# A decoder trunk on one core: three of eight weight chunks are split by other engines

## The chip, the cores and the metric

The kernel runs on one core of a Trainium2 chip. The metric is the device time of one launch in microseconds (us). A core has a matrix engine (PE, with its weight loads shown apart as PEld), a vector engine (DVE), an activation engine (ACT), a general engine (POOL), and queues that only issue DMAs (SP; ACT and POOL can issue them too). Each engine runs its own list of instructions in order, and waits on semaphores for the others.

## The reference, cut to what matters

Two layers of a decoder for 256 tokens of width 2048, all in float32. One wide projection feeds three token mixers (latent attention, a spatial gating unit, gated linear attention), whose outputs are gated, projected and merged, and projected once more onto the residual:

```
h = rms_norm(x, norm_g);  proj = h @ w_in          # 2048 -> 14416 columns
y_a, y_b, y_c = three mixers, each times silu(z)   # 1024 columns each
merged = sum_b sigmoid(gate_b) * (y_b @ w_branch[b])
x = x + merged @ w_out
```

Nearly all of the work is a product of 256 token rows with a weight matrix that is read from memory once. The precision asked for is float32's.

## The kernel before, in words

Tokens are the rows of every product: 256 tokens are two tiles of 128 (`t` = 0, 1). Weights stream past them. The host lays all weights out as one sequence of **chunks** of 128 partitions x 1024 float32 (512 KB): two contraction tiles of 128 rows by 512 output columns. There are 636 such chunks, 318 in a layer, and four narrow ones of 128 x 768. A block (`block`, L191) is one output stripe of 512 columns, made of 8 chunks (2 or 4 where the contraction is shorter).

PE multiplies in the reduced type float32r. So each chunk is split in two parts whose sum is the float32 value (`Weights.chunk`, L48): SP loads `wraw` (L64); ACT writes `whi`, the rounded value (L65); DVE writes `wlo = wraw - whi` (L66). The tokens are split in the same manner. Each contraction tile and token tile then takes three matmuls, L207 (high x high), L208 (token high x `wlo`) and L209 (token low x `whi`), so a chunk is 12 matmuls of 512 columns. L207 is first, so `whi` is needed first and `wlo` one matmul later.

The buffers rotate: four `wraw`, three `whi`, three `wlo`. `whi` of a chunk can be written when PE has finished the chunk three places before; `wraw` can be loaded when the subtraction of the chunk four places before is done.

A scheduler writes each engine's list in advance. The split is emitted with a high priority (`SPLIT_OFF`), so it stands ahead of other work in the lists of ACT and DVE. The rest (attention, transposes, the scan) is emitted in small steps between the products of a block (`step`), so that its latency is hidden behind them. POOL has little to do: the power that makes a reciprocal square root (`rsqrt`, L126, results `r_x`, `r_c`, `r_q`, `r_k`, `r_v`, `r_o`), and a few DMAs: `wa_raw`, `ba`, `vg`, `wsT`, and `x` in and out (L363, L364, L691, L693, L794, L803).

In the order of chunks a layer has the latents (chunks 1 to 16), two narrow chunks, a gate (17 to 32), the products of the latents (33 to 46, whose left operand is `cT`), then queries and keys of the scan (47 to 62, left operand `xT` again), values (63 to 78, the accumulators that become `vc`), and so on to the output projection (287 to 318). The second layer repeats this from chunk 319 on.

Of the kernel before, what the change touches and what calls it, by code (L numbers as in the profile page):

```python
# [9 lines left out]
F32 = mybir.dt.float32  # L10
# [3 lines left out]
ALU = mybir.AluOpType  # L14
# [15 lines left out]

# The tokens' order on the chip: the second half of the sequence runs backwards, so that the
# keys of the two halves' decay blocks fill the two halves of one stationary operand.
_ROWS = np.concatenate([np.arange(P), np.arange(S - 1, P - 1, -1)])

# Column blocks of the input projection, in the order in which they are computed.
_COL = dict(cq=0, ckv=512, kr=1024, za=1088, u=2112, v=3136, zb=4160, qc=5184, kc=5696,
# [3 lines left out]
class Weights:  # L40
    """Streams weight chunks in the order of the packed DRAM tensor and splits each into two
    float32r parts whose sum is the float32 value."""

    def __init__(self, nc, tc, pools, big, small):
        self.nc, self.tc = nc, tc
        self.raw, self.hi, self.lo = pools
        self.big, self.small = big, small
        self.nb = self.ns = 0  # L48

    def chunk(self, kts, ncols):  # L50
        nc, n = self.nc, kts * ncols
        if ncols == 512:
            src = self.big[self.nb]
            self.nb += 1
        else:
            src = self.small[self.ns]
            self.ns += 1
        step = 512 if ncols == 512 and self.nb <= 2 else n
        with self.tc.high_priority(offset=SPLIT_OFF):
            raw = self.raw.tile([P, 1024], F32, tag="wraw", name="wraw")  # L60
            hi = self.hi.tile([P, 1024], F32R, tag="whi", name="whi")
            lo = self.lo.tile([P, 1024], F32R, tag="wlo", name="wlo")
            for c in (slice(o, o + step) for o in range(0, n, step)):
                nc.sync.dma_start(raw[:, c], src[:, c])  # L64
                nc.scalar.activation(hi[:, c], raw[:, c], AF.Copy)  # L65
                nc.vector.tensor_tensor(lo[:, c], raw[:, c], hi[:, c].bitcast(F32), ALU.subtract)  # L66
        return ([hi[:, k * ncols:(k + 1) * ncols] for k in range(kts)],
                [lo[:, k * ncols:(k + 1) * ncols] for k in range(kts)])
# [3 lines left out]
def trunk(ctx: ExitStack, tc: tile.TileContext, a, out):  # L72
    """The trunk: tokens are the rows of the products, the split weights stream past them."""
    nc = tc.nc
    pool = lambda name, bufs, **k: ctx.enter_context(tc.tile_pool(name=name, bufs=bufs, **k))
    const = pool("const", 1)
    wraw, whi, wlo = pool("wraw", 4), pool("whi", 3), pool("wlo", 3)
    k8, k4, k2 = pool("k8", 12), pool("k4", 8), pool("k2", 5)
# [25 lines left out]

# [1 line left out]
    def load(name, shape, dt=F32):  # L106
# [10 lines left out]
    gains = first_in[:, 0:64].rearrange("p (l i) -> p l i", l=DEPTH)  # L117
    # Per layer: norm_g 0:16, cq_g 16:20, ckv_g 20:24, q_g 24, k_g 25, o_g 26:28.
    def gain(l, i, n=1):
# [11 lines left out]
    def rotary_tables():  # L131
        """cos and sin of positions * inv_freq, times the gains, per layer and for q and k."""
        posf = const.tile([P, NT], F32, name="posf")
# [24 lines left out]
        V.tensor_scalar(cos, cos, -2.0, 1.0, ALU.mult, ALU.add)  # L158
        # tables[l][q or k]: (x1, x2) -> x * TA + swap(x) * TB
        rg = t2("rope_g")[:, 0:256]  # L160
# [12 lines left out]

    # Small work (attention, transposes) is emitted in steps between the products of the blocks,
    # so that its latencies are hidden behind them.
    work, pending = [], set()
# [16 lines left out]

    def block(lhs, kts, before=None):
        """acc[t] = lhs^T @ the next weight block: three products of 12-bit parts."""
        acc = [pA(f"acc{t}") for t in range(NT)]
        for kt in range(0, kts, 2):
# [3 lines left out]
            for k, (wh, wl) in enumerate(zip(hs, ls)):  # L201
# [3 lines left out]
                for t in range(NT):  # L205
                    o, c = acc[t], slice(t * P, (t + 1) * P)
                    nc.tensor.matmul(o, xh[:, c], wh, start=kt + k == 0, stop=False)  # L207
                    nc.tensor.matmul(o, xh[:, c], wl, start=False, stop=False)  # L208
                    nc.tensor.matmul(o, xl[:, c], wh, start=False, stop=kt + k == kts - 1)  # L209
                    step()  # L210
        return acc

    def narrow_block(lhs, kts, ncols):
        """The next narrow weight block, transposed: [ncols, S]."""
        acc = pA("accT")
# [11 lines left out]
    def split(hi, lo, src, scale):  # L227
        """hi + lo = src * scale in float32r parts."""
        act(hi, src, AF.Copy, scale=scale)
        V.scalar_tensor_tensor(lo, src, scale, hi.bitcast(F32), ALU.mult, ALU.subtract)  # L230

    def hl(tiles):
        """Per k-tile (hi, lo, key) of tiles laid out [P, hi/lo, 4, S]."""
        v = [(t.rearrange("p (h k s) -> p h k s", h=2, k=4), id(t)) for t in tiles]
        return [(t[:, 0, k, :], t[:, 1, k, :], of) for t, of in v for k in range(4)]

    def transpose2(src, b):
        """Two transposed 128-column blocks of [P, NT, n]: [128, (block, token)]."""
        p = pB("ptr")
# [6 lines left out]
    def transpose_split(src, scale, name):  # L246
        """[P, NT, 512] token-major -> one k8 tile of 4 k-tiles, split; scale(k) or a number."""
        dst = t8(name, F32R)
# [20 lines left out]

# [1 line left out]
    xT = []  # L271
# [36 lines left out]
    for l in range(DEPTH):  # L308
# [14 lines left out]

# [1 line left out]
        ssr = ts("ssr")  # L325
# [10 lines left out]

# [1 line left out]
        cq8 = t8("cq")  # L338
# [13 lines left out]

# [1 line left out]
        acc = narrow_block(lhs, KT, 96)  # L354
        krT = t2("krT")
        V.tensor_copy(krT[0:64, 0:S], acc[0:64, 0:S])
        # The rank is small: the three products of parts share one contraction.
        arT = sm.tile([96, S], F32R, tag="arT", name="arT", bufs=1)
# [12 lines left out]
        def decay():  # L371
# [9 lines left out]
            for t in range(NT):  # L381
                # log-sigmoid, token-major
                p = pB("pz")
# [11 lines left out]
        def gate_silu(dst):  # L395
            """dst = z (1 + tanh(z rstd / 2)): silu(z rstd) is dst rstd / 2."""
            for j in range(2):
# [9 lines left out]

# [1 line left out]
        lq, lk = hl([cT[0]]), hl([cT[1]])  # L409
# [30 lines left out]

        # rotary: q per head, k once per token
        def rotate(dst, tmp, src, j, shape):
            """dst = src * TA + swap(src) * TB over [P, NT, heads, 64]."""
            TA, TB = tabs[:, l, j, 0], tabs[:, l, j, 1]
# [29 lines left out]
        def attention():  # L474
# [12 lines left out]
            def scores(i, h0):  # L487
                """Exponentials of the masked scores of two heads, whose rotary products fall on the same
                row tile."""
                nk = (i + 1) * P  # L490
# [61 lines left out]

# [1 line left out]
        qk = t8("qk").rearrange("p (j t c) -> p j t c", j=2, t=NT)  # L554
# [5 lines left out]
        for j in range(2):  # L560
            acc = block(lhs, KT)
            for t in range(NT):
# [5 lines left out]

        # diagonal of the attention
        dg = ts("dg", 8)  # L570
# [12 lines left out]
        def gla():  # L583
            yield from pause(4)
            # cumulative decay, feature-major [k, (h, t)]
            for hp in range(2):
# [15 lines left out]
            def factors(lv):  # L602
                """exp(ref - b) k for the keys and exp(b - ref) q for the queries of a level: no
                exponent is positive. Level 0 is the pair of chunks; the others are the pairs of
                halves of blocks within a chunk, the keys of chunk 0 being the first halves and
                those of chunk 1, which runs backwards, the second ones."""
                X = t4("X").rearrange("p (j h s) -> p j h s", j=2, h=4)
# [71 lines left out]

# [1 line left out]
        def gelu(dst, acc, t):  # L681
            """dst = p (1 + tanh(...)): gelu(p rstd) is dst rstd / 2."""
            g2 = t2("g2")
# [63 lines left out]

# [1 line left out]
        gates = {}  # L749
# [34 lines left out]

# [1 line left out]
        lm = hl(mT)  # L786
# [20 lines left out]
def _lay_out(i):  # L807
    """The inputs in the order in which the program reads them; nothing is computed."""
    g = {k: np.asarray(v) for k, v in i.items()}
    big, small = [], []  # L810

    def tiles(w, kts):
        """[K, n] -> chunks [P, kts * n]."""
        k, n = w.shape
# [78 lines left out]
```

## Time and profile before

| what | value |
|---|---|
| median of 2 runs | 1891.13 us (both 1891.13) |
| span of the profiled execution | 1889.1 us |
| PE busy | 1877.6 us, 99% of the span |
| PEld, DVE, ACT, POOL busy | 1547.6, 1097.3, 931.7, 39.6 us |
| memory traffic | 354.19 MB, 187 GB/s over the span |

The page of the profile names no time of its own for the profiled execution but the span from its first to its last instruction, 1889.1 us; the median of the runs lies 2.0 us above it. In the rows below an entry such as "L208 PE MATMUL acc<-wlo,xT" is line, engine, operation, and what it writes from what; buffer numbers are left out of names. A busy time of PE overlaps from one matmul to the next, since they are pipelined, so the pace of matmuls is read from their starts.

### The profile page before, as it was taken

What the parts mean: (1) busy time and instruction counts of PE and PEld (TensorE: products, weight loads), DVE (VectorE), ACT (ScalarE), POOL (GpSimd) and SP (SyncE); (2) the same over time, 40 slices, a digit from 0 to 9 for tenths busy, and PEclk for the clock granted to TensorE, in tenths of its full rate; (3) what the DMA queues carried; (4) which work ended last, traced back from release to release, by engine and by line L of the source; (5) the groups of instructions that cost most, each with busy time, mean ns of one, the idle gap of its engine ahead of it and who ended that gap; (6) DMA issues with size and microseconds to landing.
All of it is one profiled execution on the core that took longest, in us unless ns stands there. A gap on an engine that the chain in (4) does not pass through costs nothing.

```text
span 1889.1 us, 22587 instructions
## 1 busy us (share of the span) xinstructions
PE 1877.6 (99%) x8632; PEld 1547.6 (82%) x8632; DVE 1097.3 (58%) x1396; ACT 931.7 (49%) x1154; POOL 39.6 (2%) x41
## 2 busy tenths in 40 slices
PE   8999999999999999999999999999999999999999
PEld 7887788888888888888888877888888888888887
DVE  6666546966544545465556665479664455454654
ACT  7764445655444444444547744455544444444443
POOL 0001000000000000000000100000000000000000
PEclk9999999999999999999999999999999999999999
DMA  8554354445555555575655544545455555555654
GB/s 317 189 193 163 135 188 167 167 167 187 179 183 197 189 192 190 193 233 198 211 195 188 190 156 145 184 165 172 166 182 180 188 190 191 197 190 200 224 201 156
DMA packets 98380, 354.19 MB, mean 187 GB/s; under 512 B 11232, under 2 KB 11904, under 8 KB 97760
## 3 DMA queue, kind: packets, MB, share of 16 engines
q1 hardware_dynamic: 94176, 339.99, 52.3%
q0 software_dynamic: 2656, 10.37, 1.7%
q10 hardware_dynamic: 1440, 2.39, 0.4%
q8 instruction: 67, 1.10, 0.2%
q14 instruction: 41, 0.34, 0.1%
HBM read 348.52 MB, written 4.19 MB: 187 GB/s over the span
## 4 chain that ended last, share of the span: by engine, by line
PE 96%; DVE 1%; issue 1%; ACT 1%; POOL 1%; DMA 0%; ACTq 0%; DVEq 0%
PE acc L207 30%; PE acc L208 30%; PE acc L209 30%; PE ptr L242 2%; PE psc L499 1%; PE plv L639 1%; DVE wlo L66 1%; PE ppv L539 1%; PE psc L496 1%; POOL r_q L126 1%; PE pmx L735 0%; PE po L662 0%; PE ppt L529 0%; PE po L660 0%; DMA first_in<-in_gx 0%
## 5 line engine op out<-in xcount | busy, mean ns | idle before, releaser
L66 DVE TENSOR_TENSOR wlo<-wraw,whi 128x1024 fp32r<-128x1024 f32 (+1 forms) x642 | 782.6, 1220 | 674.1 <-ACT whi L65 672.9
L65 ACT ACTIVATE whi<-wraw 128x1024 fp32r<-128x1024 f32 (+1 forms) x642 | 677.6, 1056 | 783.1 <-PE acc L209 733.7
L207 PE MATMUL acc<-whi,xT 128*128 128x512 f32 x1792 | 723.9, 405 | 5.6 <-ACT whi L65 5.6
L208 PE MATMUL acc<-wlo,xT 128*128 128x512 f32 x1792 | 699.8, 391 | 1.5 <-DVE wlo L66 1.4
L209 PE MATMUL acc<-whi,xT 128*128 128x512 f32 x1792 | 700.3, 391 | 0.0
L207 PEld LDWEIGHTS acc<-whi,xT 128*128 128x128 f32 x1792 | 337.5, 188 | 74.3 <-ACT whi L65 5.6
L209 PEld LDWEIGHTS acc<-whi,xT 128*128 128x128 f32 x1792 | 336.8, 188 | 71.2
L208 PEld LDWEIGHTS acc<-wlo,xT 128*128 128x128 f32 x1792 | 337.9, 189 | 64.4 <-DVE wlo L66 4.0
L207 PE MATMUL acc<-whi,mT 128*128 128x512 f32 x256 | 100.5, 393 | 0.0
L209 PE MATMUL acc<-whi,mT 128*128 128x512 f32 x256 | 99.7, 389 | 0.0
L208 PE MATMUL acc<-wlo,mT 128*128 128x512 f32 x256 | 99.6, 389 | 0.0
L209 PEld LDWEIGHTS acc<-whi,mT 128*128 128x128 f32 x256 | 48.0, 188 | 10.1
L207 PEld LDWEIGHTS acc<-whi,mT 128*128 128x128 f32 x256 | 48.1, 188 | 9.7
L208 PEld LDWEIGHTS acc<-wlo,mT 128*128 128x128 f32 x256 | 48.1, 188 | 9.6
L207 PE MATMUL acc<-whi,yTa 128*128 128x512 f32 x128 | 50.2, 392 | 0.0
L209 PE MATMUL acc<-whi,yTa 128*128 128x512 f32 x128 | 49.8, 389 | 0.0
L208 PE MATMUL acc<-wlo,yTa 128*128 128x512 f32 x128 | 49.8, 389 | 0.0
L207 PE MATMUL acc<-whi,yTb 128*128 128x512 f32 x128 | 49.8, 389 | 0.0
L208 PE MATMUL acc<-wlo,yTb 128*128 128x512 f32 x128 | 49.8, 389 | 0.0
L209 PE MATMUL acc<-whi,yTb 128*128 128x512 f32 x128 | 49.8, 389 | 0.0
L207 PE MATMUL acc<-whi,yTc 128*128 128x512 f32 x128 | 49.8, 389 | 0.0
L208 PE MATMUL acc<-wlo,yTc 128*128 128x512 f32 x128 | 49.8, 389 | 0.0
(236 smaller groups left out, 1496.2 us busy)
## 6 DMA issues: line engine op xcount, KB each, us to landing
wraw<-in_w_big SPq DMA_DIRECT2D x634, 512.0 KB, 3.3
x<-x POOLq DMA_DIRECT2D x8, 512.0 KB, 4.0
x<-in_x SPq DMA_DIRECT2D x2, 1024.0 KB, 8.9
wsT<-in_w_sT POOLq DMA_DIRECT2D x2, 1024.0 KB, 5.1
x<-in_x POOLq DMA_DIRECT2D x4, 512.0 KB, 5.9
out<-x ACTq DMA_DIRECT2D x8, 256.0 KB, 4.7
xTraw<-in_gx SPq DMA_DIRECT2D x3, 512.0 KB, 7.6
wraw<-in_w_small SPq DMA_DIRECT2D x4, 384.0 KB, 3.6
```

Source lines behind the costliest of these rows:

```text
L65: nc.scalar.activation(hi[:, c], raw[:, c], AF.Copy)
L66: nc.vector.tensor_tensor(lo[:, c], raw[:, c], hi[:, c].bitcast(F32), ALU.subtract)
L126: nc.gpsimd.tensor_tensor(r[:, :n], m[:, :n], neghalf[:, :n], ALU.pow)
L207: nc.tensor.matmul(o, xh[:, c], wh, start=kt + k == 0, stop=False)
L208: nc.tensor.matmul(o, xh[:, c], wl, start=False, stop=False)
L209: nc.tensor.matmul(o, xl[:, c], wh, start=False, stop=kt + k == kts - 1)
L242: nc.tensor.transpose(p[:, k * S + t * P:k * S + (t + 1) * P], src[:, t, (b + k) * P:(b + k + 1) * P], ident)
L496: nc.tensor.matmul(o, qTn[:, h * S + i * P:h * S + (i + 1) * P], kTn[:, h * S:h * S + nk], start=True, stop=False)
L499: nc.tensor.matmul(o, qTr[rr, c + i * P:c + (i + 1) * P], kTr[rr, c:c + nk], start=False, stop=True)
L539: nc.tensor.matmul(po[:, (h - hh) * P:(h - hh + 1) * P], pT[:, k:k + P], vv[:, j, h * P:(h + 1) * P], start=j == 0, stop=j == i)
L639: nc.tensor.matmul(p[:, h * P:(h + 1) * P], X[:, 0, h, :], X[:, 1, h, :], start=True, stop=True)
```

## The change

`Weights.split` now chooses how a chunk is split by its number in the stream (`nb`, from 1), modulo 8, from chunk 9 on:

- remainder 0: DVE writes both parts, `whi` by a copy and `wlo` by the subtraction (80 chunks, two of them narrow);
- remainder 2: ACT writes `whi`, POOL does the subtraction (79 chunks);
- remainder 6: ACT writes `whi` and also `-whi` into `wlo`, and a DMA issued by POOL adds `wraw` onto `wlo` (80 chunks, two of them narrow);
- the other five as before.

The pools change from four `wraw` and three `wlo` to three `wraw` and four `wlo`. One block (the first of the values, layer 1) issues each of its 96 matmuls as two of 256 columns. Comments are taken out, which moves line numbers: the split is L57 (`whi` by ACT), L59 (POOL), L61 and L62 (ACT and the adding DMA) in the changed kernel.

```diff
+    def split(self, hi, lo, raw):
+        nc = self.nc
+        way = self.nb % 8 if self.nb > 8 else 1
+        if way == 0:
+            nc.vector.tensor_copy(hi, raw)
+        else:
+            nc.scalar.activation(hi, raw, AF.Copy)
+        if way == 2:
+            nc.gpsimd.tensor_tensor(lo, raw, hi.bitcast(F32), ALU.subtract)
+        elif way == 6:
+            nc.scalar.activation(lo, raw, AF.Copy, scale=-1.0)
+            nc.gpsimd.dma_start(lo, raw, accum_op=ALU.add)
+        else:
+            nc.vector.tensor_tensor(lo, raw, hi.bitcast(F32), ALU.subtract)
...
                 nc.sync.dma_start(raw[:, c], src[:, c])
-                nc.scalar.activation(hi[:, c], raw[:, c], AF.Copy)
-                nc.vector.tensor_tensor(lo[:, c], raw[:, c], hi[:, c].bitcast(F32), ALU.subtract)
+                self.split(hi[:, c], lo[:, c], raw[:, c])
...
-    wraw, whi, wlo = pool("wraw", 4), pool("whi", 3), pool("wlo", 3)
+    wraw, whi, wlo = pool("wraw", 3), pool("whi", 3), pool("wlo", 4)
...
-    def block(lhs, kts, before=None):
+    def block(lhs, kts, before=None, halves=1):
...
-                    o, c = acc[t], slice(t * P, (t + 1) * P)
-                    nc.tensor.matmul(o, xh[:, c], wh, start=kt + k == 0, stop=False)
-                    nc.tensor.matmul(o, xh[:, c], wl, start=False, stop=False)
-                    nc.tensor.matmul(o, xl[:, c], wh, start=False, stop=kt + k == kts - 1)
+                    c = slice(t * P, (t + 1) * P)
+                    ns = [slice(i * 512 // halves, (i + 1) * 512 // halves) for i in range(halves)]
+                    for x_, w_, first_, last_ in ((xh, wh, kt + k == 0, False), (xh, wl, False, False),
+                                                  (xl, wh, False, kt + k == kts - 1)):
+                        for n in ns:
+                            nc.tensor.matmul(acc[t][:, n], x_[:, c], w_[:, n], start=first_ and n.start == 0,
+                                             stop=last_, skip_group_check=halves > 1)
...
-            acc = block(lhs, KT)
+            acc = block(lhs, KT, halves=2 if l == 0 and j == 0 else 1)
```

The list of ACT around a chunk of remainder 6, in the first gates of layer 1. The chunk is 182, the last of its block; before, its `whi` is the third row:

```order
L65 ACTIVATE whi_4537<-wraw_4536 128x1024
L65 ACTIVATE whi_4555<-wraw_4554 128x1024
L65 ACTIVATE whi_4573<-wraw_4572 128x1024
L65 ACTIVATE whi_4596<-wraw_4595 128x1024
L65 ACTIVATE whi_4614<-wraw_4613 128x1024
```

```order
L57 ACTIVATE whi_4654<-wraw_4653 128x1024
L57 ACTIVATE whi_4672<-wraw_4671 128x1024
L61 ACTIVATE wlo_4691<-wraw_4689 128x1024
L57 ACTIVATE whi_4690<-wraw_4689 128x1024
L57 ACTIVATE whi_4714<-wraw_4713 128x1024
```

In the change the negated part of chunk 182 (`wlo_4691`) stands ahead of its own `whi_4690`, right behind the `whi` of the chunk before it.

Nearby, in the third group of gates (chunks 212 to 214), two reads of finished accumulators stand between the rows of the split:

```order
L65 ACTIVATE whi_5160<-wraw_5159 128x1024
L756 ACTIVATE gate0_5136<-acc0_4976,rs_333 128x512
L65 ACTIVATE whi_5178<-wraw_5177 128x1024
L756 ACTIVATE gate0_5136<-acc1_4977,rs_333 128x512
L65 ACTIVATE whi_5196<-wraw_5195 128x1024
```

```order
L57 ACTIVATE whi_5281<-wraw_5280 128x1024
L774 ACTIVATE gate0_5257<-acc0_5096,rs_333 128x512
L57 ACTIVATE whi_5299<-wraw_5298 128x1024
L774 ACTIVATE gate0_5257<-acc1_5097,rs_333 128x512
L61 ACTIVATE wlo_5318<-wraw_5316 128x1024
L57 ACTIVATE whi_5317<-wraw_5316 128x1024
```

Here the negated part of chunk 214 comes behind both reads. Of the 80 negated parts, 60 have no other work between the two `whi` ahead of them, 5 have one such instruction and 15 have two or more.

The list of POOL in the second layer, at the end of the products of the latents (`wlo_8461` is chunk 362, `wlo_8598` chunk 366, `wlo_8695` chunk 370):

```order
L363 DMA wa_raw_7751<-in_w_a 96x512
L364 DMA ba_7753<-in_b_a 128x512
L126 TENSOR_TENSOR r_q_8402<-m_q_8400,neghalf_87 128x16
L126 TENSOR_TENSOR r_k_8406<-m_k_8404,neghalf_87 128x16
L691 DMA vg_9634<-in_v_g 128x1024
```

```order
L62 DMA wlo_8380<-wraw_8378 128x1024
L59 TENSOR_TENSOR wlo_8461<-wraw_8459,whi_8460 128x1024
L141 TENSOR_TENSOR r_q_8544<-m_q_8542,neghalf_87 128x16
L62 DMA wlo_8598<-wraw_8596 128x1024
L141 TENSOR_TENSOR r_k_8548<-m_k_8546,neghalf_87 128x16
L59 TENSOR_TENSOR wlo_8695<-wraw_8693,whi_8694 128x1024
```

The adding DMA of chunk 366 now stands behind the power `r_q`, and the subtraction of chunk 370 behind `r_k`.

## Rows read from the trace of the kernel before

**Rows 1.** The page: busy us, share of the span, instructions; below, the granted clock by slice.
```profile
PE 1877.6 (99%) x8632; PEld 1547.6 (82%) x8632; DVE 1097.3 (58%) x1396; ACT 931.7 (49%) x1154; POOL 39.6 (2%) x41
...
PEclk9999999999999999999999999999999999999999
```

**Rows 2.** The page: the chain that ended last, shares of the span by engine.
```profile
PE 96%; DVE 1%; issue 1%; ACT 1%; POOL 1%; DMA 0%; ACTq 0%; DVEq 0%
```

**Rows 3.** Groups by line: busy us, mean ns of one, idle before and what ended it.
```profile
L207 PE MATMUL acc<-whi,xT 128*128 128x512 f32 x1792 | 723.9, 405 | 5.6 <-ACT whi L65 5.6
L208 PE MATMUL acc<-wlo,xT 128*128 128x512 f32 x1792 | 699.8, 391 | 1.5 <-DVE wlo L66 1.4
...
L65 ACT ACTIVATE whi<-wraw 128x1024 fp32r<-128x1024 f32 x634 | 671.8, 1060 | 777.6 <-PE acc L209 728.5 <-issue 37.4 <-ACT smx L513 2.5
L756 ACT ACTIVATE gate<-acc,rs 128x512 f32<-128x512 f32 x48 | 32.6, 679 | 24.9 <-PE acc L209 24.9
...
L66 DVE TENSOR_TENSOR wlo<-wraw,whi 128x1024 fp32r<-128x1024 f32 x634 | 776.0, 1225 | 670.6 <-ACT whi L65 669.6
```

**Rows 4.** Timeline of ACT, then DVE, 557 to 570 us: start, duration, instruction.
```profile
557.71 1.06 ACT L65 ACTIVATE whi<-wraw 128x1024 fp32r<-128x1024 f32 x1 [1.66 <-PE acc L209]
...
558.80 1.23 DVE L66 TENSOR_TENSOR wlo<-wraw,whi 128x1024 fp32r<-128x1024 f32 x1 [1.49 <-ACT whi L65]
```

**Rows 5.** Timeline of PE, 562.7 to 566 us: two chunks' first matmuls.
```profile
562.95 0.39 PE L207 MATMUL acc<-whi,xT 128*128 128x512 f32 x1
563.18 0.39 PE L208 MATMUL acc<-wlo,xT 128*128 128x512 f32 x1
...
565.67 0.39 PE L207 MATMUL acc<-whi,xT 128*128 128x512 f32 x1
565.90 0.39 PE L208 MATMUL acc<-wlo,xT 128*128 128x512 f32 x1
```

**Rows 6.** Groups by line, POOL: the powers.
```profile
L126 POOL TENSOR_TENSOR r_k<-m_k,neghalf 128x16 f32<-128x16 f32 x2 | 5.8, 2896 | 0.0
L126 POOL TENSOR_TENSOR r_x<-m_x,neghalf 128x2 f32<-128x2 f32 x2 | 1.4, 720 | 27.8 <-DVE m_x L124 27.8
```

**Rows 7.** DMA issues: count, KB each, median us from issue to landing.
```profile
wraw<-in_w_big SPq DMA_DIRECT2D x634, 512.0 KB, 3.3
x<-x POOLq DMA_DIRECT2D x8, 512.0 KB, 4.0
wsT<-in_w_sT POOLq DMA_DIRECT2D x2, 1024.0 KB, 5.1
```

**Rows 8.** All that touches wraw: shortest, median and longest landing.
```profile
DMA to landing us min/median/max: 2.7/3.3/8.7
```

**Rows 9.** Timeline of all engines but PE, 560 to 576 us: SP's loads.
```profile
560.06 13.93 SPq L64 DMA_DIRECT2D wraw<-in_w_big  x6
```

**Rows 10.** Timelines of SP, DVE and PE near the start: loads and fourth chunk.
```profile
4.93 3.37 SPq L64 DMA_DIRECT2D wraw<-in_w_big  x2
14.98 2.35 DVE L66 TENSOR_TENSOR wlo<-wraw,whi 128x1024 fp32r<-128x1024 f32 x2
16.38 0.39 PE L208 MATMUL acc<-wlo,xT 128*128 128x512 f32 x1
```

**Rows 11.** Timeline of POOL, 1075 to 1095 us.
```profile
1080.24 4.98 POOL L126 TENSOR_TENSOR r_q<-m_q,neghalf 128x16 f32<-128x16 f32 x1 [82.95 <-DVE m_q L124]
```

**Rows 12.** Timeline of PE, 1082.2 to 1085.6 us: from the latents' products to chunk 366.
```profile
1082.08 0.39 PE L209 MATMUL acc<-whi,cT 128*128 128x512 f32 x1
1082.31 0.39 PE L207 MATMUL acc<-whi,xT 128*128 128x512 f32 x1
...
1085.26 0.39 PE L208 MATMUL acc<-wlo,xT 128*128 128x512 f32 x1
```

**Rows 13.** Timeline of PE, 52 to 53 us: the narrow block's matmuls of 256 columns.
```profile
52.03 0.28 PE L221 MATMUL accT<-xT,whi 128*96 128x256 f32 x1
52.15 0.27 PE L222 MATMUL accT<-xT,whi 128*96 128x256 f32 x1
```

**Rows 14.** Groups by line, PEld: a weight load of the wide blocks.
```profile
L208 PEld LDWEIGHTS acc<-wlo,xT 128*128 128x128 f32 x1792 | 337.9, 189 | 64.4 <-DVE wlo L66 4.0
```

## The prediction, made before the changed kernel was run

> **What bounds the kernel now.** I read the busy shares first [rows 1], then the chain of waits [rows 2]: PE is busy 99% of the span and holds 96% of the chain. The other engines have room (DVE 58%, ACT 49%, POOL 2%). Next the groups by line [rows 3]: before its main matmuls PE waited 5.6 us once for ACT (the start) and 1.5 us for DVE, while ACT's `whi` spent most of its 777.6 us of idle time waiting for PE to free a buffer. So the split runs ahead of PE and is paced by it. The sizes come from two timelines [rows 4, 5]. Two chunks start at 562.95 and 565.67, so a chunk lasts 2.72 us (12 matmuls, 0.227 each). The `whi` begun at 557.71 belongs to the chunk that starts at 562.95: with three `whi` it starts when the chunk three before has ended, and two chunks lie between. Its `wlo` ends at 558.80 + 1.23 = 560.03 and is first used at 563.18. Slack of an ordinary split: **3.15 us**. A split may get that much slower at no cost; what exceeds it stops PE, once per chunk split that way.
>
> The median of the runs, 1891.1, lies 2.0 above the profiled span of 1889.1, and I add my terms to 1891.1. Nothing here can be gained: PE's own waits above come to 7 us, and a change must save 38 us to pass 2%, which is about what a measurement of this kernel can tell from no change.
>
> **Remainder 0 (DVE writes both parts).** The DVE copy of 128x1024 is not in the trace. From below it is free. From above I take DVE's subtraction of the same shape, 1.23 us [rows 3], against 1.06 on ACT: the pair ends 0.2 later of 3.15. Cost 0. DVE loses 159 subtractions (195 us) and gains at most 80 copies (98 us), ACT gives 80 and takes 80. The cover for all of this is the slack, and both engines keep theirs.
>
> **Remainder 2 (POOL subtracts).** ACT's part ends at 558.77 in the picture above, the first use is at 563.18: POOL has **4.4 us**. The nearest row is the same operation and shape on DVE, 1.23 us [rows 3]; I take 0 as long as POOL needs under 3.6 times that. The far end: POOL's only arithmetic in the trace is a power, 0.72 us for 2 columns and 2.90 for 16 [rows 6], 0.156 us a column, which for 1024 columns would be 160 us and add 12 ms in 79 chunks. A power is another operation; I keep that end for the tail alone.
>
> **Remainder 6 (ACT negates, a DMA adds).** In the list of ACT the negated part stands right behind the `whi` of the chunk before, so it starts a chunk earlier than an ordinary `wlo`. Put on the timeline: if that `whi` is the one of 557.71, the negated part takes 558.77 to 559.83, and the chunk's first use of `wlo` is 565.90 [rows 4, 5]. The DMA has **6.07 us** from POOL's issue to its landing. No DMA of that kind is in the trace. Nearest below is a plain 512 KB from POOL, 4.0 us [rows 7]. But adding reads `wlo` as well as `wraw`, 1 MB, and POOL's load of 1 MB lands in 5.1 us, in the same weight traffic [rows 7]. Far above: if the old `wlo` has to be read before the writing starts, two transfers end to end, 4.0 + 3.3 = 7.3 us [rows 7], and the longest landing of any `wraw` is 8.7 [rows 8]. I take 5.1, since the bytes read are those of that row. For the 60 chunks with nothing between the rows of ACT, 5.1 is under 6.07: cost 0. The 5 with one instruction between lose about 0.7 [rows 3] and still fit. For the 15 with two or more, 1.4 to 2 us of the budget go to reads of accumulators at 0.68 each [rows 3]: 4.7 to 4.1 remain, 0.4 to 1.0 is missing where both reads fall due just then. I put down **+6**.
>
> That the DMA reads twice the bytes is my inference from the row of 1 MB. The Trainium skill says it outright ("Collectives: The Full Stack", section "The bandwidth ceiling: the fold count and why AG ≠ RS ≠ AR"): an add in the DMA path takes two source reads on one ring and runs at about half the rate of a copy. By a plain copy's 4.0 us the +6 above would be 0; by this rule it stands. No run here has shown it yet.
>
> **Buffers.** A `wraw` loaded at 560.06, when a subtraction ended [rows 9], lands 3.3 later [rows 7], at 563.4. With three buffers it feeds the `whi` of 565.87 instead of the one of 568.59: 2.5 us early, no cost. The adding DMA holds `wraw` until it lands, to about 565; the next load, SP's later ones behind it, then lands at 568.2 and is due at 568.59. Cover enough at 5.1 us; at 8 it would come 2.5 late, which the slack of 3.15 still hides. At the start there is no such cover: SP issues the fourth chunk's load at 4.93, and its subtraction ends at 16.20 for a first use at 16.38 [rows 10]. With three buffers that load waits about 3 us for the first subtraction. The bounds are 0 (the loads there queue on each other anyway) and 5; I take **+2**.
>
> **POOL's list.** In the second layer the adding DMA of chunk 366 stands behind `r_q`, which ends at 1080.24 + 4.98 = 1085.22 [rows 11]; landing 5.1 later, 1090.3, against the chunk's first use at 1085.26 [rows 12] (latents' products end at 1082.08, chunk 365 starts at 1082.31, 366 one chunk on). **+5**, bounds 0 and 6. Elsewhere POOL's old work falls between two of its new items, four chunks (10.9 us) apart, and the DMAs it issues wait for things already done there. The 159 new instructions take POOL nothing that anyone else needs.
>
> **The halved block.** 96 matmuls of 0.227 become 192. The narrow block's matmuls of 256 columns start 0.12 us apart [rows 13]: 2 x 0.118 - 0.227 = 0.009, +0.9 us. The far end, every weight load of 0.189 [rows 14] in the open, is 192 x 0.189 - 96 x 0.227 = +14.5. I take **+1**, the load there running under the matmul before it.
>
> Sum: 1891.1 + 6 + 2 + 5 + 1 = **1905 us**.
>
> **The rivals.**
>
> *The adding DMA lands too late (slower).* Place: PE waiting at L208 in one chunk of eight. It decides from 6.07 us on in the 65 clear chunks and from about 4.5 in the other 15. At 7.3 us: 65 x 1.23 + 15 x 2.8 = 122 us, with the other +8 **2021 us**; at 6.2 the sum is 1932, which is where 2% begins; at 8.0, 2078. For it: I have only reads of memory as a price, and reading, adding and writing back may cost more, while one weight load always runs beside it. Against: the row of 1 MB, with 1 us to spare. 40%.
>
> *POOL's subtraction is too slow (slower).* From 4.4 us on, 79 x the excess: at 6 us +126, **2031**. The Trainium skill sharpens this ("SBUF — State Buffer", "Who interferes with whom"): a DVE instruction with two inputs in SBUF and a POOL instruction that reads SBUF exclude each other for a whole instruction. As a mechanism here, POOL first waits out a DVE subtraction of 1.23 us and the point falls from 4.4 to 3.2 us. By that rule the time with POOL at 4.4 us is 1905 + 79 x 1.23 = 2002. The trace, where POOL never subtracts, shows neither way. 6%.
>
> *POOL's list blocks more than once (slower).* Other waits on POOL, such as `r_k` at 2.9 us, delay an item in front of them: some eight such places, up to 5 us each, 1945. 4%.
>
> *The change does nothing on the path, and less work on DVE helps.* The waits that could vanish are 7 us: 1884 at best, inside 2%. 2%; over 2% faster, 1%.
>
> **How the numbers follow.** My forecast, 1905 us with its own range 1890 to 1929, has 47%. With the 2% above, a result within 2% (1853 to 1929) gets 0.50 when a little of the late DMA just under 6.2 us is counted in; slower 0.49; faster 0.01. The range of 8 in 10 must reach into the late DMA, up to a landing of about 8 us: **1890 to 2070**. It leaves out a DMA of 8.7 us and more, and a very slow POOL.
>
> **What would show it.** Right: PE's idle time before L208 stays under some 15 us in all, the adding DMA lands in 5 to 6 us, POOL's subtraction under 4.4. The chunk behind `r_q` in layer 2 waits about 5 us. The 192 halves start 0.12 us apart. Wrong: a wait of L208 for a landing, about 80 times, with equal length; or for POOL L59, 79 times; or the granted clock, 9 tenths or more in every slice now [rows 1], falling behind such waits.

## The result, and the profile after

The changed kernel took 2000.72 us (median of 2 runs, 1999.38 to 2002.07) against 1891.13: 1.058 times as long, interval 1.0549 to 1.0611. The forecast of 1905 was wrong; the time lies inside the range, at the place where the first rival, the adding DMA that lands too late, had put it. The profiled execution spans 1997.6 us, 108.5 more than before.

The page of the changed kernel: busy time and share of each engine, then granted clock by slice, then the chain that ended last, by engine (its shares add up to 47%: it is followed back no further):

```profile
PE 1911.7 (96%) x8728; PEld 1556.9 (78%) x8728; DVE 991.9 (50%) x1317; ACT 922.4 (46%) x1154; POOL 299.5 (15%) x200
...
PEclk9999999999999999999999999999999999999999
...
PE 32%; DMA 11%; ACT 2%; issue 2%; DVE 0%; POOL 0%; ACTq 0%; POOLq 0%
```

PE fell from 99% [rows 1] to 96%: idle time went from 11.5 us (1889.1 less 1877.6) to 85.9, and its busy time rose by 34. The chain, 96% PE before [rows 2], now holds one part of DMA for every three of PE. What PE waited for is in its own list of waits (waiting line, what it waited for, us in total, times, longest):

```profile
PE acc L226 <- DMA wlo<-wraw: 63.2, 54, 3.2
PE acc L226 <- ACT whi L57: 6.9, 2, 5.7
PE acc L226 <- DVE wlo L64: 3.8, 3, 2.5
...
PE acc L226 <- POOL wlo L59: 0.6, 1, 0.6
```

One row is new and large: the landing of the adding DMA. POOL's subtraction cost PE 0.6 us, once, and the old waits for ACT and DVE [rows 3] stayed small. All that touches `wlo` (duration in ns, shortest/median/longest), and the landing of the adding DMA:

```profile
L64 DVE TENSOR_TENSOR wlo<-wraw,whi x483: 684/1226/2272, 5.7 to 1986.5; 128x1024 fp32r<-128x1024 f32 x159, 128x512 fp32r<-128x512 f32 x2
...
L61 ACT ACTIVATE wlo<-wraw x80: 847/1050/1064, 39.0 to 1965.4; 128x1024 fp32r<-128x1024 f32 x78, 128x768 fp32r<-128x768 f32 x2
L62 POOL DMA_DIRECT2D wlo<-wraw x80: 845/872/935, 40.6 to 1967.0; - x80
L59 POOL TENSOR_TENSOR wlo<-wraw,whi x79: 2358/2387/3731, 30.8 to 1981.1; 128x1024 fp32r<-128x1024 f32 x79
...
DMA to landing us min/median/max: 4.5/6.0/8.1
```

It lands 4.5 us after its issue at best and 6.0 in the middle, where the prediction had taken 5.1. The other DMAs became slower too: these are the rows of the page that answer to [rows 7].

```profile
wraw<-in_w_big SPq DMA_DIRECT2D x634, 512.0 KB, 3.9
...
x<-x POOLq DMA_DIRECT2D x8, 512.0 KB, 5.8
wsT<-in_w_sT POOLq DMA_DIRECT2D x2, 1024.0 KB, 8.9
```

**One late chunk.** Chunk 190, one turn of eight behind chunk 182, whose lists of ACT stand in the section on the change, shows the whole chain. From the timelines of DVE, SP, ACT, POOL and PE, with start, duration, instruction, and in brackets the idle time before it and what ended that:

```profile
607.39 1.23 DVE L64 TENSOR_TENSOR wlo<-wraw,whi 128x1024 fp32r<-128x1024 f32 x1 [1.54 <-ACT whi L57]
...
608.64 0.33 SPq L80 DMA_DIRECT2D wraw<-in_w_big  x1
...
607.49 1.06 ACT L61 ACTIVATE wlo<-wraw 128x1024 fp32r<-128x1024 f32 x1
...
609.08 0.88 POOL L62 DMA_DIRECT2D wlo<-wraw  x1 [7.46 <-PE acc L226]
...
613.98 0.61 PE L226 MATMUL acc<-whi,xT 128*128 128x512 f32 x2
616.30 0.50 PE L226 MATMUL acc<-wlo,xT 128*128 128x512 f32 x1 [1.70 <-DMA wlo<-wraw]
```

The negated part ends at 607.49 + 1.06 = 608.55. POOL issues the DMA at 609.08, 0.53 us later, a step that the prediction had left out. (The bracket names PE, whose semaphore moved last, at 608.95; ACT's had moved at 608.56, and the instruction in which POOL waited for it ended at 608.59.) In between, at 608.64, the subtraction of the chunk before has ended (607.39 + 1.23 = 608.62) and SP issues a weight load into the `wraw` that it freed. The two transfers run together: the load lands after 5.17 us, the adding DMA after 7.17, at 616.25. The two high matmuls begun at 613.98 are the last of the chunk before and the first of this one; the `wlo` matmul was due at about 613.98 + 2 x 0.227 = 614.43 and starts at 616.30.

**Where the 108.5 us are.** I sorted PE's matmuls into chunks and took what each chunk's period (from its first matmul to the next chunk's) exceeds 2.72 us by, by remainder modulo 8. Chunks of remainder 6 exceed it by 113.1 us together, against 20.2 before: 92.9 of the 108.5. (Chunk 334 is left out, since two narrow chunks follow it before the next; it gained 1.3 us.) Of these, 73.9 lie ahead of the chunk's first `wlo` matmul, some 7 are the slower start of the matmul behind the wait (0.09 us in each of 80), and the rest, about 12, lie between the matmuls after it. The other seven remainders gained 14.3 us together, the largest 4.6 (remainder 0).

Much of the 12, and some of what the other chunks gained, is the clock. The longest wait, 3.19 us, is that of chunk 366; from POOL's and PE's timelines there:

```profile
1140.13 3.86 POOL L141 TENSOR_TENSOR r_q<-m_q,neghalf 128x16 f32<-128x16 f32 x1 [7.79 <-DVE m_q L139]
1143.95 0.85 POOL L62 DMA_DIRECT2D wlo<-wraw  x1
...
1144.69 0.61 PE L226 MATMUL acc<-whi,xT 128*128 128x512 f32 x2
1148.51 0.52 PE L226 MATMUL acc<-wlo,xT 128*128 128x512 f32 x1 [3.19 <-DMA wlo<-wraw]
1148.84 1.03 PE L226 MATMUL acc<-whi,xT 128*128 128x512 f32 x2
1149.67 0.63 PE L226 MATMUL acc<-wlo,xT 128*128 128x512 f32 x1
```

The adding DMA stands behind `r_q`, as predicted. After the wait two matmuls take 0.83 us (1148.84 to 1149.67) instead of 0.45. The same place by stretches of time (busy us and count of each engine, then the granted clock, the DMA share and GB/s):

```profile
1142.00:1145.00 3.00, 3.00 (x15) 2.42 (x13) 0.98 (x3) 2.04 (x3) 3.00 (x3) 1.00 0.17 70
1148.50:1152.00 3.50, 3.50 (x9) 2.80 (x10) 3.50 (x4) 0.00 (x0) 0.00 (x0) 0.55 0.54 165
1152.00:1158.00 6.00, 6.00 (x27) 4.64 (x26) 4.85 (x4) 2.12 (x2) 1.17 (x1) 0.98 0.43 147
```

The granted clock falls from 1.00 to 0.55, that is from the level of 2.4 GHz to that of 1.2 for most of the stretch, and is back by 1152. The changed kernel's trace has eight such stretches, 27.3 us together, seven of them behind waits of 1.9 to 3.2 us for the adding DMA; the kernel before has one, at its very end. At half pace the eight cost about 14 us. In the page's row of slices they are too short to be seen; the mean granted clock of the run, 0.993, holds them.

### The profile page after: what moved, and what is told of

Its sections match the earlier page's. It is cut to its first block, busy times and chain, and to the rows that moved or that the text cites. A ratio compares the mean times of both kernels' runs of the same rounds, so it can differ in the third digit from the quotient of the medians.

```text
span 1997.6 us, 22976 instructions
## 1 busy us (share of the span) xinstructions
PE 1911.7 (96%) x8728; PEld 1556.9 (78%) x8728; DVE 991.9 (50%) x1317; ACT 922.4 (46%) x1154; POOL 299.5 (15%) x200
## 3 DMA queue, kind: packets, MB, share of 16 engines
q10 hardware_dynamic: 1440, 2.39, 0.3%
## 5 line engine op out<-in xcount | busy, mean ns | idle before, releaser
L226 PE MATMUL acc<-whi,xT 128*128 128x512 f32 (+1 forms) x3648 | 1181.4, 395 | 5.7 <-ACT whi L57 5.7
L64 DVE TENSOR_TENSOR wlo<-wraw,whi 128x1024 fp32r<-128x1024 f32 (+2 forms) x483 | 591.0, 1225 | 711.4 <-ACT whi L57 708.8
L57 ACT ACTIVATE whi<-wraw 128x1024 fp32r<-128x1024 f32 (+2 forms) x562 | 592.4, 1055 | 752.8 <-PE acc L226 444.3
L226 PE MATMUL acc<-wlo,xT 128*128 128x512 f32 (+1 forms) x1824 | 707.2, 391 | 41.2 <-DMA wlo<-wraw 37.7
L59 POOL TENSOR_TENSOR wlo<-wraw,whi 128x1024 fp32r<-128x1024 f32 x79 | 191.1, 2419 | 908.4 <-ACT whi L57 897.1
L62 POOL DMA_DIRECT2D wlo<-wraw x80 | 69.9, 873 | 629.4 <-ACT wlo L61 416.6
L61 ACT ACTIVATE wlo<-wraw 128x1024 fp32r<-128x1024 f32 (+1 forms) x80 | 83.8, 1048 | 23.5 <-DMA wraw<-in_w_big 21.5
L226 PE MATMUL acc<-whi,cT 128*128 128x512 f32 x224 | 70.6, 395 | 0.0
L55 DVE CAST whi<-wraw 128x1024 fp32r<-128x1024 f32 (+1 forms) x80 | 55.2, 690 | 30.5 <-PE acc L226 26.1
L226 PEld LDWEIGHTS acc<-wlo,mT 128*128 128x128 f32 x256 | 48.1, 188 | 21.0 <-DMA wlo<-wraw 11.5
L226 PEld LDWEIGHTS acc<-whi,yTc 128*128 128x128 f32 x256 | 50.5, 197 | 12.3 <-ACT whi L57 1.6
```

What stands on the lines that cost most here:

```text
L55: nc.vector.tensor_copy(hi, raw)
L57: nc.scalar.activation(hi, raw, AF.Copy)
L59: nc.gpsimd.tensor_tensor(lo, raw, hi.bitcast(F32), ALU.subtract)
L61: nc.scalar.activation(lo, raw, AF.Copy, scale=-1.0)
L62: nc.gpsimd.dma_start(lo, raw, accum_op=ALU.add)
L64: nc.vector.tensor_tensor(lo, raw, hi.bitcast(F32), ALU.subtract)
```

## The experiments

The theory that the profile suggests (A in the texts): the loss is the adding DMA's, which lands after the 6.07 us that the prediction had granted it. The rivals: the pools with one `wraw` fewer (B), small parts that add up (C), and the second read of the addition. For the later runs theory A is split: a collision with one weight load (A1) against a fixed price of 6 us (A2), with loads that bunch because there are only three `wraw` (B2) as the rival. Every kernel below is the changed one with the edit shown, and was timed beside the kernel before on the same chip (1891.05 us for the first four, 1891.02 for the others).

**1. Without the adding DMA.** Chunks of remainder 6 are split as ordinary ones; all else is kept.

```diff
-        elif way == 6:
+        elif way == 99:
```

> The changed kernel with remainder 6 split the ordinary way (ACT rounds, DVE subtracts); remainders 0 and 2, the pools of 3 wraw and 4 wlo and the halved block stay. Theory A (the adding DMA lands about 0.9 us after PE wants its wlo, 80 times, and PE restarts slowly after each wait): 109 less 93 us, about 1907 us, and no wait of a matmul for a landing of wlo. Theory B (three wraw instead of four make the loads of raw weights late, and with them everything behind): most of the 109 us stays, 1970 to 2000. Theory C (all small parts add up): 1940 to 1960.

Measured: 1897.02 us, ratio 1.0031 (1.002 to 1.0043). PE's waits, as above:

```profile
PE acc L226 <- ACT whi L57: 5.6, 1, 5.6
PE acc L226 <- DVE wlo L64: 5.6, 6, 2.7
PE acc L226 <- POOL wlo L59: 0.4, 1, 0.4
```

Theory A had asked for about 1907. So the DVE copies, POOL's 79 subtractions, the pools and the halved block cost 6 us together, and the adding DMA 2000.7 - 1897.0, about 104.

**2. The adding DMA alone**, with the changed pools; the copy, POOL's subtraction and the halves undone.

```diff
-        way = self.nb % 8 if self.nb > 8 else 1
+        way = 6 if self.nb > 8 and self.nb % 8 == 6 else 1
```

> The changed kernel with only remainder 6 split in the new way; remainders 0 and 2 ordinary, no halved block, pools of 3 wraw and 4 wlo stay. Theory A: 1891 + 93 = 1984 us, 1975 to 1995. Theory B: also near 1990, since the pools stay, but with the waits on loads of wraw and not on landings of wlo. Theory C: 1930 to 1960.

Measured: 1984.59 us, ratio 1.049 (1.0463 to 1.0518), as theory A had it, and what PE waits for is the landing of `wlo`, as in the changed kernel:

```profile
PE acc L226 <- DMA wlo<-wraw: 59.7, 55, 3.2
```

The landing is no shorter with POOL free of subtractions:

```profile
L64 DVE TENSOR_TENSOR wlo<-wraw,whi x562: 683/1225/1264, 5.4 to 1971.6; 128x1024 fp32r<-128x1024 f32 x185, 128x512 fp32r<-128x512 f32 x2, 128x768 fp32r<-128x768 f32 x1
...
DMA to landing us min/median/max: 4.5/6.6/8.5
```

POOL issues here 0.29 us after the negated part ends, not 0.53. The trace shows what differs: in all 80 turns of this run POOL's wait for ACT stands in the DMA instruction itself; in 78 of the 80 of the changed kernel it stands in an instruction of its own ahead of the DMA (0.53 us), and in the other 2 in the DMA instruction (0.29 again). The earlier issue wins nothing, since it moves the DMA just ahead of the load: 45 of the 80 have no load within the 1 us before them but one within the 1 us after (39 of these within 0.1 us), and they land in 6.6 us. A load that starts with the DMA delays it whichever of the two is first.

The row of DVE is for a later point: DVE's longest subtraction is 1.26 us where POOL subtracts nothing, 2.27 where it does.

**3. The old pools**, four `wraw` and three `wlo`.

```diff
-    wraw, whi, wlo = pool("wraw", 3), pool("whi", 3), pool("wlo", 4)
+    wraw, whi, wlo = pool("wraw", 4), pool("whi", 3), pool("wlo", 3)
```

> The changed kernel with the pools of before: 4 wraw, 3 wlo. Theory A: the negated part must now wait for PE to free the wlo of three chunks before instead of four; it starts 2.72 us later, saves the 1.06 us of the whi that stood ahead of it, so PE waits about 1.6 us longer in each of 80 chunks: 2000 + 130 = 2130 us, 2090 to 2160. Theory B: loads come a chunk earlier, 1900 to 1950. The two go opposite ways.

Measured: 1980.29 us, ratio 1.0479 (1.0458 to 1.05). Both expectations missed, and the reason is the finding of the study. With three `wlo` the negated part does start 1.4 us later, near the 1.6 of theory A: from its end to the due time of the first `wlo` matmul there are 4.63 us in the middle chunk instead of 6.09. But the landing became shorter:

```profile
DMA to landing us min/median/max: 4.5/4.7/8.1
```

The later issue meets another moment of the loads. In this kernel 61 of the 80 adding DMAs are issued 1 to 2 us after the last weight load, and land in 4.59 us in the middle; in the changed kernel 41 are issued within 0.5 us of one (6.09 us) and 20 within 0.5 to 1 us (6.70). So the 6 us are not the price of the DMA by itself, and theory A had to be cut in two: 4.5 us of its own, and some 1.5 us from the load that starts with it. The time stays near 1980 because what the landing won, the start lost: 0.53 + 4.6 is still over the 4.63 that are left, and PE waits as long as before:

```profile
PE acc L226 <- DMA wlo<-wraw: 60.2, 65, 3.7
```

**4. A plain copy in its place**: the DMA is issued at the same place, without the addition.

```diff
-            nc.gpsimd.dma_start(lo, raw, accum_op=ALU.add)
+            nc.gpsimd.dma_start(lo, raw)
```

> The changed kernel with the DMA of remainder 6 as a plain copy of wraw onto wlo, without the addition; all else stays (the low part of these chunks is then the whole weight, so the result is not the reference's). If the second read that the addition needs is what makes it late, a copy lands in about 4.4 to 5 us instead of 6.0, the wait at the first wlo falls from 0.9 to 0.2 us or none, 1905 to 1930 us. If it is the way through POOL and SBUF at all (0.53 us from ACT to POOL's issue, 0.87 of issue, the traffic), it lands in 5.5 to 6 us and the time stays at 1975 to 2000.

Measured: 1935.03 us, ratio 1.0236 (1.0211 to 1.0261), between the two expectations, as is the landing.

```profile
L62 POOL DMA_DIRECT2D wlo<-wraw x80: 528/562/607, 41.2 to 1904.2; - x80
...
DMA to landing us min/median/max: 2.9/5.2/7.3
```

At its shortest the addition costs 4.5 - 2.9 = 1.6 us, and 0.31 us more to issue (872 less 562 ns). Even the plain copy is stretched by 2.3 us in the middle, so the collision does not depend on the addition; with a wait for the landing of 19.1 us instead of 63.2 it still makes the kernel over 2% slower. But 66 of the 109 us went with the addition: its 1.6 us is as much needed for the loss as the collision.

**5. The load that collides cut to an eighth.** The load released by the subtraction of a chunk of remainder 5 is that of remainder 0, issued 0.44 us ahead of the adding DMA at 608.64 above. Here it brings 128 of the 1024 columns, which the split reads eight times.

```diff
+                if ncols == 512 and self.nb > 8 and self.nb % 8 == 0:
+                    nc.sync.dma_start(raw[:, 0:128], src[:, 0:128])
...
+                    self.split(w(hi), w(lo), raw[:, 0:128].unsqueeze(1).broadcast_to([P, 8, 128]))
+                    continue
```

> The changed kernel, but of the chunks of remainder 0 only the first 128 columns are loaded (64 KB instead of 512) and used eight times over (the result is not the reference's). That load is the one that starts with the adding DMA: it goes out when the subtraction of the chunk before remainder 6 ends. Theory A1 (the adding DMA needs 4.5 us by itself, and 1.5 us more while it shares the engines with one weight load): in the chunks with nothing in ACT's way it lands in about 4.6 us, under the 5.5 us that are left of the 6.07 after 0.53 for the way from ACT to POOL; the wait at the first wlo falls from 74 us to 10 to 25 us, about 1910 to 1930 us. Theory A2 (6 us is its own price in this place, whatever else moves): the landing stays at 6 us, 1985 to 2000 us.

Measured: 1928.27 us, ratio 1.0194 (1.0178 to 1.0209). The landing, and PE's first wait:

```profile
DMA to landing us min/median/max: 4.5/4.6/6.9
```

```profile
PE acc L231 <- DMA wlo<-wraw: 14.3, 12, 3.2
```

The short load is still issued at the same moment (597.52, the adding DMA at 597.94 in one chunk):

```profile
597.52 0.33 SPq L81 DMA_DIRECT2D wraw<-in_w_big  x1
...
597.94 0.88 POOL L62 DMA_DIRECT2D wlo<-wraw  x1 [7.44 <-PE acc L231]
```

With its bytes gone, the landing is 4.6 and the time ahead of the first `wlo` matmul falls from 73.9 to 17.3 us. As theory A1 had it, 72 of the 109 us went with one load in eight. As in run 4, taking away either part of the landing brings most of it back under the budget; neither is the cause alone. The run also moves some 36 MB less, a tenth of the traffic; that the gain comes from the load beside the DMA, and not from less traffic at large, rests on run 3, where the full loads stay and the landing is 4.7, and on the moments of issue: in the changed kernel and runs 2, 3, 6 and 7 together, 281 adding DMAs have a load issued within 1 us on either side and land in 6.6 us in the median, and the other 119 in 5.1.

**6. Four `wraw` and four `wlo`**, made room for by smaller pools elsewhere (`k2` 4, scores 4).

```diff
-    wraw, whi, wlo = pool("wraw", 3), pool("whi", 3), pool("wlo", 4)
+    wraw, whi, wlo = pool("wraw", 4), pool("whi", 3), pool("wlo", 4)
```

> The changed kernel with four wraw and four wlo; to make room, two smaller pools lose buffers (k2 from 5 to 4, the scores from 6 to 4). Theory A1: one load still starts with the adding DMA, only it is the next chunk's, so landing stays near 6 us and the wait near 0.9 us a chunk; what goes is the lateness of wraw (the negation waited 21 us for loads, the whi 250 us behind the waits): 1960 to 1995 us. Theory B2 (the landing is late because three wraw make the loads bunch): landing falls to about 4.7 us as with the pools of before, 1900 to 1925 us.

Measured: 1998.34 us, ratio 1.056 (1.0525 to 1.0596), no better; theory A1 had asked for 1960 to 1995 and a landing near 6 us.

```profile
DMA to landing us min/median/max: 4.5/6.2/8.8
```

The negated parts start on time (in the median 1.44 us after the start of the last matmul of the chunk four before, against 1.57 in the changed kernel, where 27 of 77 had waited for their own `wraw`; here none does), and 61 of the 80 DMAs have a load issued within the 0.5 us ahead, against 41. A fourth buffer gives the load another chunk to fetch, not another moment. That refutes the rival of the pools.

**7. DVE also writes `whi` of remainder 5**, to let ACT negate earlier.

```diff
-        if way == 0:
+        if way in (0, 5):
```

> The changed kernel where DVE also writes whi of remainder 5, so that the negation of remainder 6 has no whi ahead of it on ACT. Theory A1: it starts up to 1.06 us earlier (as far as its wraw has landed), so the addition starts ahead of the weight load instead of with it, and lands earlier by 0.5 to 1.5 us against a use that does not move: the wait falls to 0.1 to 0.5 us a chunk, 1915 to 1960 us. Theory A2, a fixed 6 us: 0.5 to 1 us less a chunk where wraw is there in time, 1930 to 1970 us. If wraw lands too late for it, no change: 1990 to 2000 us.

Measured: 1984.59 us, ratio 1.0504 (1.0476 to 1.0533).

```profile
DMA to landing us min/median/max: 4.6/6.6/8.6
```

The negated part starts at about the same point in the median (1.51 us after that matmul; 0.26 in the earliest tenth), so ACT's list was not what held it, and the collision stays. ACT's own list of waits says what did, the landing of the chunk's `wraw`, in 61 cases:

```profile
ACT wlo L61 <- DMA wraw<-in_w_big: 164.9, 61, 6.2
```

This is the third case of the expectation, a `wraw` that lands too late, with a time just under its 1990.

**8. The addition in two halves**, two DMAs of 512 columns, the first half being all that the chunk's first six matmuls need.

```diff
-            nc.gpsimd.dma_start(lo, raw, accum_op=ALU.add)
+            n = lo.shape[-1] // 2
+            for c in (slice(0, n), slice(n, 2 * n)):
+                nc.gpsimd.dma_start(lo[:, c], raw[:, c], accum_op=ALU.add)
```

> The changed kernel with the adding DMA cut in two, one for each contraction tile (512 columns); the second half is needed six matmuls (1.36 us) after the first. Both theories: the first half moves half the bytes, so it lands about 1 us earlier than the whole (near 5 us), and the second, issued 0.6 to 0.9 us later, lands near 6.5 us when it has 1.36 us more: the wait of 0.9 us a chunk falls to 0.1 to 0.5 us, 1920 to 1960 us. If the fixed part of a DMA sets the landing and not its bytes, the first half lands at 5.5 us or more and little is won: 1965 to 2000 us.

Measured: 1956.14 us, ratio 1.0335 (1.0318 to 1.0352).

```profile
DMA to landing us min/median/max: 3.3/5.0/7.8
```

A half lands in 5.0 us in the middle instead of 6.0, and the time ahead of the first `wlo` matmul in these chunks falls to 20.0 us; some 2.7 come back ahead of the second half. The time lies inside the first expectation. It is the best of the versions that keep the adding DMA and all the loads, and 59 us slower than the version of run 1. No version tried beats the kernel before.

## Why the prediction was wrong

**The failed step** is in the part on remainder 6: "I take 5.1, since the bytes read are those of that row", and from it "5.1 is under 6.07: cost 0" for the clear chunks. From the end of the negated part the changed kernel needs 0.53 + 6.05 = 6.6 us in the median, where 6.09 are there. Three things make up the miss:

- *The collision, 1.5 us.* With the load cut (run 5) the DMA lands 4.57 us after its issue and 5.10 after the end of the negated part, hand-over included. That this is the 5.1 of the prediction is luck: the price was 0.5 too high for the DMA by itself, and the hand-over that it left out is as long. The collision was at nothing in the sum. I had taken the row of `wsT` [rows 7] as measured "in the same weight traffic". The traffic was the same, the moment was not: its two issues, at 231.5 and 1171.5 us, come 3.47 us behind a load and 1.71 ahead of the next, and say nothing of a transfer that starts 0.44 us behind a load, up to 1 us in 61 of its 80 turns. My own timeline held this: the negated part of 558.77 to 559.83 ends just before the load issued at 560.06 [rows 4, 9]. Of the rival I wrote "one weight load always runs beside it", and gave that no price.
- *The hand-over from ACT to POOL, 0.53 us*, was left out of the sum; without the collision the price that was too high would have covered it.
- *The tight chunks.* I counted 60 clear, 5 with one instruction ahead and 15 with more. By the trace 44 have 6.0 us or more, 17 between 5.5 and 6.0, 12 between 4.5 and 5.5, and 7 less. Their waits ahead of the first `wlo` matmul are 22.8, 23.1, 14.7 and 13.3 us. With the collision gone (run 5) these groups lose 0.3, 1.4, 9.4 and 6.2: so even by the right landing the +6, with chunk 366 left apart, would have been 14 (17.3 less 3.4).

The trace of the kernel before did hold a hint of the collision. POOL's eight loads of 512 KB at L794 land there after:

```profile
DMA to landing us min/median/max: 4.4/5.3/6.9
```

The two that a weight load precedes by 0.18 us land in 6.4 and 6.9 us (another DMA of POOL's, issued 1.8 us before, runs beside them too). POOL's stores of the same size (L803), issued 1.25 us ahead of a load, land in 3.4 to 3.5. The median of 4.0 [rows 7] hid that spread.

On top come the restarts and the stretches at half clock, some 19 us; the clock I had named as a sign of being wrong, but priced neither.

**What held.** Each other term is near its size. *Chunk 366*: predicted +5; its first `wlo` came 3.4 us late, and 5.1 were lost there in all with the slow stretch. The mechanism was right and the size luck: `r_q` took 3.86 us there and not 4.98, the DMA 4.5 and not 5.1, and the clock, which I had not counted, made up for both. *The halves*: predicted +1, measured 0.7, by the sum of the starts in that block. *The start*: predicted +2; in run 1, 1.25 us by chunk 11. *The copy by DVE*: costed at 0 with 1.23 us as upper bound; it takes 0.69 (55.2 us in 80). *POOL's subtraction*: costed at 0 below 4.4 us; it takes 2.39 in the median (L59 above), 1.95 times DVE's 1.23. Of the 0 for the splits, 4 us came back in run 1 as waits for DVE (5.6 instead of 1.5).

**The two rules.** The Trainium skill states ("Collectives: The Full Stack", "The bandwidth ceiling: the fold count and why AG ≠ RS ≠ AR") that an add in the DMA path needs two source reads and runs at about half the rate of a copy. The trace agrees in direction: 4.5 us against 2.9 at the shortest, 1.6 times. It gave no hint of the loss, since 4.5 and the hand-over of 0.53 fit the budget.

The Trainium skill also states ("SBUF — State Buffer", "Who interferes with whom") that a DVE instruction with two inputs in SBUF and a POOL instruction that reads SBUF contend for a port that one holds at a time. The trace shows DVE standing still behind POOL: its longest subtraction, 2.27 us where run 2 has 1.26 at most, overlaps the end of one on POOL,

```profile
883.27 2.40 POOL L59 TENSOR_TENSOR wlo<-wraw,whi 128x1024 fp32r<-128x1024 f32 x1 [12.95 <-ACT whi L57]
...
884.48 2.27 DVE L64 TENSOR_TENSOR wlo<-wraw,whi 128x1024 fp32r<-128x1024 f32 x1 [1.28 <-ACT whi L57]
```

and ends 1.08 us after it, not far from a whole DVE subtraction. Five of DVE's 483 took over 1.3 us. The other way round it shows less: in run 1 three POOL subtractions of 2.90 us each had a whole DVE subtraction beside them, and were 0.5 us longer than the median of 2.39. POOL's longest, 3.73, overlaps other DVE instructions and no subtraction of a chunk. With 2.39 + 1.23 = 3.6 under the 4.4, all this cost PE 0.6 us.

**The chances.** The rival that came true had 40%, and its decision point, 6.07 us, was right to 0.02 (6.09). At 6.6, hand-over included, its own formula gives 65 x 0.53 + 15 x 2.1 = 66 us, with the other +8 1965: of the right kind, 36 short of 2001. (Two of its other sums are 1 us off: by the formula 6.2 gives 1933 and 8.0 gives 2077.) Of the 36 some 18 are the restarts and the clock in chunks of remainder 6, some 13 what the other chunks lost beyond the +3 for the start and the halves, and the rest the tight chunks.

## What to carry to other kernels

Price a new DMA by the moment at which it starts, not by a row of another DMA that started at another one, nor by a median that hides the spread: look on the timeline for what the same instructions release at that moment, here a load freed by the neighbouring chunk's subtraction. When a step changes engines, count the hand-over as part of its budget. Where the spare time of a periodic wait is smaller than the spread of landings in the trace (here 2.7 to 8.7 us for one kind of load [rows 8]), forecast the late side, since each miss stops PE and the longer ones let its clock fall.

## What the runs showed of the hardware

- An accumulating DMA of 128 x 1024 float32 from one buffer on the core onto another: 4.5 us from issue to landing at best, against 2.9 for a plain copy of the same shape; 872 ns of POOL to issue it, against 562.
- Beside one weight load of 512 KB it takes about 1.5 us longer (4.6 with that load cut to 64 KB, 6.0 with it whole), and the median of all loads is 0.6 longer (3.3 to 3.9). The load may start just ahead of it or just behind (6.6 us in run 2). Issued 1.4 us later, it landed 1.3 us sooner after its issue (run 3).
- From the end of ACT's write to the issue on POOL 0.53 us pass where POOL's wait for ACT stands in an instruction ahead of the DMA (78 of 80 in the changed kernel), and 0.29 where it stands in the DMA instruction itself (the other 2, and all of runs 2 and 7).
- A DVE copy of float32 into the reduced type, 128 x 1024, takes 0.69 us in the changed kernel, less than ACT's 1.06 for the same.
- After a wait of 3.19 us PE was granted 0.55 of its clock over the next 3.5 us, in which each matmul took about 0.42 us instead of 0.227.
